# Weights read ahead, a norm chain in a fixed order and transposes moved among products, at the seam between an output projection and a SwiGLU FFN

## The chip, the core and the metric

The kernel runs on one core of a Trainium2 chip. The core has five engines with a queue each: PE (TensorE: matmuls and transposes into PSUM banks, and the loads of its stationary operand, which the profile lists apart as PEld), DVE (VectorE), ACT (ScalarE), POOL (GpSimd) and SP (SyncE, which here issues nearly all transfers). An engine takes the instructions of its queue in the order in which they stand; between engines, semaphores say when an operand is ready or a buffer is free. The metric is the device time of one execution in microseconds (us): the median of several runs.

## The reference

One encoder layer for 512 tokens of width 1024. Three mixers work on the same normalised input (sparse attention, stick-breaking attention, attention to memory), and their gated sum is `merged`. What the change touches comes after that:

```
x = x + rmsnorm(merged @ w_out, g_mix_post)
h = rmsnorm(x, g_ffn_pre)
gu = h @ w_ffn_in                       # 1024 x 5632
f = (silu(gu[:, :2816]) * gu[:, 2816:]) @ w_ffn_out
x = x + rmsnorm(f, g_ffn_post)
```

All values are float32.

## The kernel before, in words

A product in float32 is made of three products of rounded parts: each operand is split into a high part (a copy by ACT, `CAST` in the trace) and a low part (the difference, by DVE, `TENSOR_TENSOR`), and PE multiplies high by high, high by low, low by high (`passes`, `split`, `parts`). So each block of 512 KB of weights costs a transfer into a raw buffer (`wraw`, `lraw` or, after the change, `act`), a cast on ACT and a subtraction on DVE, each over 128x1024, before PE may use it. Buffers come from pools with a fixed number of places: `act` has 22, `wraw` 3, `lraw` 2, `wh` and `wl` 2 each, `w2` (both parts in one tile) 4. A split into a place that is taken waits until PE has used what is there. There are 8 PSUM banks.

`mix_out` (L785) multiplies the 512 tokens by `w_out` in two halves of 256 tokens; tokens come in tiles of 128, called 0 to 3 here. `w_out` has 8 blocks of 128 rows, k0 to k7, used alternately through a pair `wh`, `wl` (even blocks) and a `w2` tile (odd blocks). The first half runs k0 to k7 for tokens 0 and 1, twelve matmuls of 512 columns for a block; the splits of k4 to k7 are kept. The second half runs the kept blocks k4 to k7 first, then k0 and k1, which are loaded and split again, and at last k2 and k3 token by token (the tail, L755), so that token 2 is done before token 3. The split of k2 in the second half goes into the `wh`, `wl` pair of k6, and so has to wait until the second half has used k6.

When a token is done, `post_norm` (L767) takes squares of its two banks (ACT), a root (a small sum on DVE, a power on POOL, two small steps on DVE: `ms`, `rs`, `rt`), two products with the gain (DVE, `prod`) and two residual sums (DVE, `fin`); `normed` (L253) takes squares, root and a scaling (`xn`) of that for the FFN. Then `to_h2` (L797) transposes `xn` by PE, 16 transposes of 128x128 for two tokens, into a bank for each of 8 blocks of features, and ACT and DVE split each bank into `h2` (L78, L79). PE's order is written by hand throughout the kernel; that of ACT, DVE, POOL and SP is chosen by a scheduler when the program is built, except where a fixed order is asked for (`manual_schedule`).

The transposes of tokens 0 and 1 are handed out among the products of the second half: after more than `FT` (14) units of product, `FR` (0.65) of them for each further unit (L811). Past 17 units (`FW`, in the tail) the first three pairs of blocks of `w_ffn_in` are asked for (L809): raw buffers from `wraw` and `lraw`, parts in twelve `act` places; the low parts of three of the six blocks are meant for POOL, of which two stand there in the order of POOL's queue (L819 passes it for columns above 2816).

`ffn` (L932) multiplies the three pairs by the first half of `h2` (144 matmuls of 256 columns), then makes the last transposes (tokens 2 and 3), three steps ahead of the products of the first pair with the second half. What follows (L830 on) is a scheme with seven products for four blocks, whose left sides (`left_sides`, L851: sums and differences of weights, more splits) DVE and ACT prepare at the same time.

Of the kernel before, what the change touches and what calls it, by code (L numbers as in the profile page):

```python
# [27 lines left out]
TAKEN = -3.4e38  # L28
REL = 640
GA, GB = 2.05, 1.85  # L30
FS, FM, GC, FC, FA, FB, FW, FT, FR = 0.7, 50, 1.8, 2.0, 1.00, 2.20, 17.00, 14, 0.65

C_AQ, C_AK, C_AV, C_IQ, C_IK, C_BQ, C_BK, C_BV, C_CQ, C_G = (
    0, 512, 1024, 1536, 2048, 2120, 2632, 3144, 3656, 4168)
# [13 lines left out]
class Layer:  # L48
    def __init__(self, ctx, tc, a):
        self.tc, self.nc, self.a = tc, tc.nc, a  # L50
        self.queue, self.owed, self.nw, self.late = [], 0.0, 0, None
        pool = lambda name, **kw: ctx.enter_context(tc.tile_pool(name=name, bufs=1, **kw))
        self.pool = pool
        self.const = pool("const")
        self.sb = pool("sb")
        self.ps = pool("ps", space=bass.MemoryType.PSUM)
        self.dram = pool("dram", space=bass.MemoryType.DRAM)
# [162 lines left out]
                self.split(*out[t], ps)  # L220


    def squares(self, halves, both=False):

        ss = self.col("ss", 2)
        for c, x in enumerate(halves):
            junk = self.sb.tile([P, 512], F32, name="junk", tag="gate", bufs=2)
# [24 lines left out]

    def normed(self, x):  # L253

        r = self.rstd(self.squares([x[:, 0:512], x[:, 512:1024]]))
        xn = self.big("act", F32)
        self.scaled(xn, x, r)
        return xn


# [470 lines left out]
    def tok_pair(self, w_src, acts, nk, toks, tail=0, keep=0):  # L731

        pss = [[self.bank() for _ in range(2)] for _ in toks]
        kept, self.kept = self.kept, {}
        order = [*kept, *(k for k in range(nk) if k not in kept)]

        def one(k, w, t, ps, cs):
            wh, wl = w  # L740
            ah, al = acts[k]
            s = slice(t * P, (t + 1) * P)
            for st_, mv_, f, l in ((ah, wh, True, False), (ah, wl, False, False), (al, wh, False, True)):
                for c in cs:
# [22 lines left out]
    def post_norm(self, ps, grow, x, store=None):  # L767

        nc = self.nc
        r = self.rstd(self.squares(ps))  # L770
        ts = []
        for c in range(2):
            t = self.sb.tile([P, 512], F32, name="prod", tag="gate", bufs=2)
            nc.vector.scalar_tensor_tensor(t, ps[c], -0.5, grow[:, c * 512:(c + 1) * 512],
                                           op0=OP.mult, op1=OP.mult)
            ts.append(t)
        for c, t in enumerate(ts):
            s = slice(c * 512, (c + 1) * 512)
            nc.vector.scalar_tensor_tensor(x[:, s], t, r, x[:, s], op0=OP.mult, op1=OP.add)
            if store is not None:  # L780
                (nc.sync, nc.scalar)[c].dma_start(store[:, s], x[:, s])

    NFIRST = 3

    def mix_out(self):  # L785
        nc, a = self.nc, self.a
        gp = self.grow("g_mix_post", "act")
        self.h2 = [self.pair("h") for _ in range(NK)]
        self.x1 = [self.load_rows(a["x"], t, "fin") for t in range(NT)]
        xn = {}  # L790
# [12 lines left out]

        self.done, self.kept = done, {}
        for pr in range(2):
            us = 0.0
            for t in self.tok_pair(a["w_out"], self.mT, NK, (2 * pr, 2 * pr + 1), tail=2 * pr, keep=4 * (1 - pr)):
                us += t
                if pr == 1 and us > FW and not self.first_ffn:  # L809
                    self.first_ffn = [self.ffn_weights(j, ("act", "act")) for j in range(self.NFIRST)]  # L810
                if pr == 1 and us > FT:  # L811
                    self.fill(FR * t / 2.56)
            if pr == 0:
                self.add(to_h2(0))
        self.drain()
# [116 lines left out]
    def ffn(self):  # L932
# [28 lines left out]
        self.gated(pss, out(0))  # L961
        y = self.right_sides()
        for j, u in enumerate(first[1:], 1):
# [37 lines left out]
```

## Time and profile before

| | us |
|---|---|
| median of 3 runs | 912.44 (912.41 to 913.62) |
| the profiled execution, its own time | 910.88 |
| its span, first to last instruction | 909.1 |
| PE busy | 888.3 (98%) |
| DVE, ACT, POOL busy | 641.5, 458.6, 117.1 |

PE is busy nearly all the time, so the time is the sum of PE's work and of the places where PE waits. In the stretch that the change touches, from the first product with `w_out` at 503.5 us to the last transposes at 577.5 us, such places are found in the order of time of PE and PEld: a row there gives in brackets how long the engine sat idle before it and who ended that.

### The profile page before, as it was taken

Reading aid. Unit: us, or ns where it says so; the run is one execution under the profiler, and the core shown is the slowest. Engines: PE = TensorE matmul, PEld = TensorE weight load, DVE = VectorE, ACT = ScalarE, POOL = GpSimd, SP = SyncE. Lnnn points to the kernel's source line nnn. Section 1 sums busy time; section 2 is a strip of 40 time slices with the busy share of each in tenths; the row PEclk is TensorE's granted clock in tenths of the full one; section 3 lists DMA queues with packets and bytes.
Section 4 is the critical chain, followed back from the end, with each engine's and each line's share of the span. In section 5 each row is a group of like instructions: output and inputs, shape, how many; then the busy total and the mean of one; then the engine's idle time right before and its main releaser. Section 6 shows DMA issues by size and latency. Waiting matters only on the chain.

```text
span 909.1 us, 13518 instructions
## 1 busy us (share of the span) xinstructions
PE 888.3 (98%) x5146; PEld 780.1 (86%) x5146; DVE 641.5 (71%) x1120; ACT 458.6 (50%) x808; POOL 117.1 (13%) x153
## 2 busy tenths in 40 slices
PE   8999999999999999999999999899999999999997
PEld 7888888888888888888788888899999999888885
DVE  6589999953688976787563478788888887932215
ACT  6465674332666665666353355455555555811111
POOL 2000000020132304433212123400000000000000
PEclk9999999999999999999999999999999999999999
DMA  6523543454354433222483624213333334533002
GB/s 203 173 83 117 168 111 93 127 128 116 104 156 112 128 82 92 70 59 58 140 252 107 185 83 127 71 47 95 115 109 102 114 97 139 164 97 106 29 1 92
DMA packets 129541, 101.17 MB, mean 111 GB/s; under 512 B 4652, under 2 KB 115292, under 8 KB 129476
## 3 DMA queue, kind: packets, MB, share of 16 engines
q1 hardware_dynamic: 128884, 99.26, 37.9%
q10 hardware_dynamic: 592, 1.05, 0.3%
q8 instruction: 40, 0.66, 0.3%
q14 instruction: 25, 0.20, 0.1%
HBM read 93.73 MB, written 2.12 MB: 105 GB/s over the span
## 4 chain that ended last, share of the span: by engine, by line
PE 82%; DVE 10%; issue 3%; ACT 2%; POOL 2%; DMA 1%; POOLq 0%; DVEq 0%; ACTq 0%
PE bank L85 19%; PE bank L86 19%; PE bank L87 19%; PE bank L745 15%; DVE wl L75 3%; PE bank L545 2%; PE bank L560 1%; PE bank L179 1%; PE bank L178 1%; PE bank L209 1%; PE bank L211 1%; PE bank L210 1%; DMA lraw<-in_w_ffn_in_dram 1%; DVE e L632 1%; POOL rs L241 1%
## 5 line engine op out<-in xcount | busy, mean ns | idle before, releaser
L75 DVE TENSOR_TENSOR wl<-wraw,wh 128x1024 fp32r<-128x1024 f32 (+1 forms) x112 | 128.5, 1149 | 101.3 <-ACT wh L74 101.0
L74 ACT CAST wh<-wraw 128x1024 fp32r<-128x1024 f32 (+1 forms) x112 | 107.2, 959 | 139.3 <-PE bank L86 74.7
L85 PE MATMUL bank<-h,wh 128*128 128x512 f32 (+1 forms) x376 | 149.0, 396 | 0.0
L87 PE MATMUL bank<-h,wl 128*128 128x512 f32 (+1 forms) x376 | 145.4, 387 | 1.0 <-DVE wl L75 0.9
L86 PE MATMUL bank<-h,wh 128*128 128x512 f32 (+1 forms) x376 | 145.1, 386 | 0.0
L745 PE MATMUL bank<-w,act 128*128 128x512 f32 x360 | 89.0, 394 | 0.0
L87 PEld LDWEIGHTS bank<-h,wl 128*128 128x128 f32 x376 | 70.6, 188 | 15.8 <-DVE wl L75 1.7
L85 PEld LDWEIGHTS bank<-h,wh 128*128 128x128 f32 x376 | 71.0, 189 | 11.6 <-issue 0.2
L86 PEld LDWEIGHTS bank<-h,wh 128*128 128x128 f32 x376 | 70.9, 188 | 11.5
L745 PEld LDWEIGHTS bank<-w,act 128*128 128x128 f32 x360 | 67.4, 188 | 14.9
L745 PE MATMUL bank<-wh,act 128*128 128x512 f32 x240 | 72.5, 393 | 0.0
L85 PE MATMUL bank<-act,wh 128*128 128x256 f32 (+1 forms) x204 | 69.3, 340 | 0.7 <-DVE s L907 0.7
L86 PE MATMUL bank<-act,wh 128*128 128x256 f32 (+1 forms) x204 | 68.0, 334 | 0.0
L87 PE MATMUL bank<-act,w 128*128 128x256 f32 x228 | 64.2, 282 | 0.0
L86 PE MATMUL bank<-act,w 128*128 128x256 f32 x228 | 64.2, 281 | 0.0
L87 PE MATMUL bank<-h,w 128*128 128x256 f32 x228 | 64.2, 281 | 0.0
L86 PE MATMUL bank<-h,w 128*128 128x256 f32 x228 | 64.2, 281 | 0.0
L85 PE MATMUL bank<-act,w 128*128 128x256 f32 x228 | 64.2, 281 | 0.0
L85 PE MATMUL bank<-h,w 128*128 128x256 f32 x228 | 64.2, 281 | 0.0
L241 POOL TENSOR_TENSOR rs<-ms,mhalf 128x1 f32<-128x1 f32 x18 | 11.6, 646 | 387.4 <-DVE ms L240 383.7
L609 POOL TENSOR_TENSOR p<-toep,score 128x128 f32<-128x128 f32 (+3 forms) x32 | 30.4, 963 | 200.2 <-DVE score L518 102.9
L745 PEld LDWEIGHTS bank<-wh,act 128*128 128x128 f32 x240 | 45.0, 188 | 9.8
(190 smaller groups left out, 2109.5 us busy)
## 6 DMA issues: line engine op xcount, KB each, us to landing
wraw<-in_w_in_dram SPq DMA_DIRECT2D x64, 512.0 KB, 3.7
lraw<-in_w_ffn_in_dram SPq DMA_DIRECT2D x22, 512.0 KB, 4.0
wraw<-in_w_ffn_in_dram SPq DMA_DIRECT2D x22, 512.0 KB, 3.7
wraw<-in_w_ffn_out_dram SPq DMA_DIRECT2D x11, 512.0 KB, 3.5
lraw<-in_w_ffn_out_dram SPq DMA_DIRECT2D x11, 512.0 KB, 3.5
wraw<-in_w_mem_kv_dram SPq DMA_DIRECT2D x8, 512.0 KB, 3.7
lraw<-in_w_out_dram SPq DMA_DIRECT2D x6, 512.0 KB, 5.5
wraw<-in_w_out_dram SPq DMA_DIRECT2D x6, 512.0 KB, 3.9
```

What stands on the lines that cost most here:

```text
L74: self.nc.scalar.copy(hi, src)
L75: (eng or self.nc.vector).tensor_tensor(lo, src, hi.bitcast(F32), op=OP.subtract)
L85: self.nc.tensor.matmul(out, lhsT=sh, rhs=mh, start=first and i == 0, stop=False, **kw)
L86: self.nc.tensor.matmul(out, lhsT=sh, rhs=ml, start=False, stop=False, **kw)
L87: self.nc.tensor.matmul(out, lhsT=sl, rhs=mh, start=False, stop=last and i == n - 1, **kw)
L178: self.nc.tensor.matmul(out, lhsT=x, rhs=y[:, 0:n], start=True, stop=False)
L179: self.nc.tensor.matmul(out, lhsT=x, rhs=y[:, T:T + n], start=False, stop=True)
L209: self.nc.tensor.matmul(ps, lhsT=ah[:, s], rhs=wh[:, k2], start=st, stop=False)
L241: self.nc.gpsimd.tensor_tensor(r, ms, self.mhalf, op=OP.pow)
L545: self.nc.tensor.transpose(ps[:, c:c + P], p[i][:, j * P:(j + 1) * P], self.ident)
L609: nc.gpsimd.tensor_tensor(s, toep[0][:, 0:n][:, ::-1], self.mask[i], op=OP.add)
L745: self.nc.tensor.matmul(ps[c], lhsT=st_[:, s], rhs=mv_[:, 0, c * 512:(c + 1) * 512], start=f and k == order[0], stop=l and k == order[-1])
```

## The change

- `ffn_weights` reads its raw block into an `act` place instead of `wraw` or `lraw`, and all low parts are made by DVE. The three pairs are asked for in the first half of `w_out`, after more than 4, 9 and 14 units (`FW`).
- The transposes of tokens 0 and 1 begin after 12 units instead of 14 (`FT`), one unit for each unit of product (`FR`).
- From the tail of the second half on (`tail`, called ahead of the loads of k2 and k3) until the first pair's products with the second half are issued, ACT, DVE and POOL keep the order in which the program is written (`manual_schedule`), and the norm chain of tokens 2 and 3 is written out step by step in it (`done`, `ends`).
- The squares write what nobody reads into `xn`, not into the two `gate` buffers; one of the two squares of `normed` for tokens 2 and 3 is done by DVE (`both`).
- The first three steps of the last transposes stand among the products: one after six of eight pieces of the third pair with the first half, one at its end, one ahead of the first pair's products with the second half.

```
-FS, FM, GC, FC, FA, FB, FW, FT, FR = 0.7, 50, 1.8, 2.0, 1.00, 2.20, 17.00, 14, 0.65
+FS, FM, GC, FC, FA, FB, FT, FR = 0.7, 50, 1.8, 2.0, 1.00, 2.20, 12, 1.0
+FW = 4, 9, 14, 99
...
+        if self.tail:
+            self.tail()
         ws = {k: load(k) for k in order[nk - tail:]}
...
+        def square(t):
+            xn[t] = self.big("act", F32)
+            ss[t] = self.squares(bank[t], to=xn[t])
...
+        def ends():
+            square(3)
+            prods(3)
+            root(3)
+            square2(2)
+            root(2)
+            residual(3)
+            square2(3)
+            scale(2)
+            root(3)
+            scale(3)
+
+        order = lambda: self.tc.manual_schedule(engines={
+            mybir.EngineType.DVE, mybir.EngineType.Activation, mybir.EngineType.Pool})
...
         def done(t, ps):
-            self.post_norm(ps, gp, self.x1[t])
-            xn[t] = self.normed(self.x1[t])
+            bank[t] = ps
+            if t < 2:
+                self.post_norm(ps, gp, self.x1[t])
+                xn[t] = self.normed(self.x1[t])
+            if t == 2:
+                square(2)
+                prods(2)
+                root(2)
+                residual(2)
+            if t == 3:
+                ends()
...
+        def tail():
+            self.ordered.enter_context(order())
...
-                if pr == 1 and us > FW and not self.first_ffn:
-                    self.first_ffn = [self.ffn_weights(j, ("act", "act")) for j in range(self.NFIRST)]
+                if pr == 0 and us > FW[len(self.first_ffn)]:
+                    self.first_ffn.append(self.ffn_weights(len(self.first_ffn)))
...
-    def ffn_weights(self, j, tags=None):
-        return [self.parts(self.load(self.a["w_ffn_in"][:, c:c + P], NK, P), tags, self.nc.gpsimd if tags and c>DFF else None) for c in (j * P, DFF + j * P)]
+    def ffn_weights(self, j):
+        return [self.parts(self.load(self.a["w_ffn_in"][:, c:c + P], NK, P, "act"), ("act", "act"))
+                for c in (j * P, DFF + j * P)]
...
-            run(products(*u, 0))
+            for i, _ in enumerate(products(*u, 0)):
+                if j == self.NFIRST - 1 and i in (5, 7):
+                    next(self.last_h2)
...
-        for k in range(NK + 2):
-            if k < NK:
+        for k in range(NK):
+            if k + 2 < NK:
                 next(self.last_h2)
-            if k > 1:
-                for ps, w in zip(pss, ws):
-                    self.feat_k(ps[:, 256:512], w, self.h2, k - 2, n=256, t0=256)
+            for ps, w in zip(pss, ws):
+                self.feat_k(ps[:, 256:512], w, self.h2, k, n=256, t0=256)
+        self.ordered.close()
```

**PE, second half of `w_out`.** Before, from the block k0 (`wh`, `wl`) and k1 (`w_5395`) to the start of the tail (k3 is `w_5433`); `ident` marks a transpose:

```order
L745 MATMUL bank<-wh,act 128x512 x2
L745 MATMUL bank<-w_5395,act 128x512 x12
L359 MATMUL bank<-ident,act 128x128 x6
L745 MATMUL bank<-wh,act 128x512
L745 MATMUL bank<-wl,act 128x512
```

and with the change:

```order
L750 MATMUL bank<-wh,act 128x512 x2
L364 MATMUL bank<-ident,act 128x128 x8
L750 MATMUL bank<-w_5447,act 128x512 x12
L364 MATMUL bank<-ident,act 128x128 x8
L750 MATMUL bank<-wh,act 128x512
```

The transposes of tokens 0 and 1 stand one block earlier, eight ahead of the twelve matmuls of k1 and eight behind; before, six followed k1 and ten were spread over the tail.

**ACT, from the squares of token 0's banks to the first squares for token 1's `xn`.** With buffer numbers; `junk` and `act_5313`, `act_5343` are what the squares write, `fin_5107` and `fin_5109` the residual sums of tokens 0 and 1, `bank_5115` to `bank_5118` their banks. Before (`wh_5377` is k0's cast, `wh_5427` k2's):

```order
L231 ACTIVATE junk_5262,ss_5259<-bank_5116 128x512
L231 ACTIVATE junk_5278,ss_5277<-fin_5107 128x512
L231 ACTIVATE junk_5280,ss_5277<-fin_5107 128x512
L231 ACTIVATE junk_5292,ss_5291<-bank_5117 128x512
L231 ACTIVATE junk_5294,ss_5291<-bank_5118 128x512
L74 CAST wh_5377<-wraw_5375 128x1024
L231 ACTIVATE junk_5310,ss_5309<-fin_5109 128x512
L74 CAST wh_5427<-wraw_5425 128x1024
```

With the change (`wh_5409` is k0's cast, `wh_5486` k2's, `w2_5492` k3's; `act_5250` and `act_5256` belong to the third FFN pair, `w2_5961` and `wh_5976` to the left sides of the next):

```order
L237 ACTIVATE junk_5298,ss_5295<-bank_5116 128x512
L76 CAST wh_5409<-wraw_5407 128x1024
L76 CAST act_5250<-act_5248 128x1024
L76 CAST wh_5486<-wraw_5484 128x1024
L76 CAST act_5256<-act_5254 128x1024
L76 CAST w2_5492<-lraw_5490 128x1024
L237 ACTIVATE act_5313,ss_5314<-fin_5107 128x512 x2
L237 ACTIVATE junk_5326,ss_5325<-bank_5117 128x512
L237 ACTIVATE junk_5328,ss_5325<-bank_5118 128x512
L76 CAST w2_5961<-wraw_5957 128x1024
L76 CAST wh_5976<-lraw_5959 128x512
L237 ACTIVATE act_5343,ss_5344<-fin_5109 128x512 x2
```

Five casts moved ahead of the squares of token 0's residual sum and two more ahead of those of token 1's; DVE has the five low parts in the same place (`wl`, `act`, `wl`, `act`, `w2`).

**DVE, the end of the norm chain of tokens 2 and 3.** Before, from the scaling of token 3 (L251) to the first split of the last transposes (L79); `wl_6069`, `wl_6070` and `wh_6081` are left sides of a later block:

```order
L251 TENSOR_SCALAR act_5583<-fin_5113,rs_5577 128x1024
L871 TENSOR_TENSOR wl_6069<-lraw_6064 128x512
L871 TENSOR_TENSOR wl_6070<-wraw_6062,lraw_6064 128x512
L871 TENSOR_TENSOR wl_6069<-wl_6069,wraw_6062 128x512
L75 TENSOR_TENSOR wh_6081<-lraw_6064,wh_6081 128x512
L871 TENSOR_TENSOR wl_6070<-wraw_6062,wl_6069 128x512
L79 SCALAR_TENSOR_TENSOR h_5099<-bank_5735,cols_96,h_5099 128x256
```

With the change:

```order
L938 TENSOR_TENSOR wl_6061<-wraw_6053,wl_6060 128x512
L257 TENSOR_SCALAR act_5507<-fin_5111,rs_5552 128x1024
L246 TENSOR_SCALAR ms_5567<-ss_5560 128x1
L77 TENSOR_TENSOR wh_6072<-lraw_6055,wh_6072 128x512
L252 SCALAR_TENSOR_TENSOR rt_5571<-rs_5568,ms_5567 128x1
L253 SCALAR_TENSOR_TENSOR rs_5568<-rt_5571,rs_5568 128x1
L257 TENSOR_SCALAR act_5536<-fin_5113,rs_5568 128x1024
L81 SCALAR_TENSOR_TENSOR h_5099<-bank_5713,cols_96,h_5099 128x256
```

The five operations on left sides that stood between the last scaling and the first split now stand ahead of it.

## Rows read from the trace of the kernel before

**Rows 1.** The page: busy time of PE, share of the span, instructions.

```profile
PE 888.3 (98%) x5146; PEld 780.1 (86%) x5146; DVE 641.5 (71%) x1120; ACT 458.6 (50%) x808; POOL 117.1 (13%) x153
```

**Rows 2.** PEld in order of time: start us, us, instruction [idle before <- who ended it].

```profile
547.27 0.20 PEld L359 LDWEIGHTS bank<-ident,act 128*128 128x128 f32 x2 [1.97 <-DVE h L79]
...
569.39 0.31 PEld L359 LDWEIGHTS bank<-ident,act 128*128 128x128 f32 x3 [0.40 <-DVE act L251]
572.80 0.20 PEld L359 LDWEIGHTS bank<-ident,act 128*128 128x128 f32 x2 [3.09 <-DVE h L79]
```

**Rows 3.** DVE in order of time, at the two places where PE waits.

```profile
539.30 0.75 DVE L251 TENSOR_SCALAR act<-fin,rs 128x1024 f32<-128x1024 f32 x1
539.97 1.22 DVE L75 TENSOR_TENSOR act<-wraw,act 128x1024 fp32r<-128x1024 f32 x1
...
542.24 4.58 DVE L75 TENSOR_TENSOR act<-wraw,act 128x1024 fp32r<-128x1024 f32 x2
546.74 1.65 DVE L79 SCALAR_TENSOR_TENSOR h<-bank,cols,h 128x256 fp32r<-128x256 f32 x4
...
569.25 0.69 DVE L871 TENSOR_TENSOR wl<-lraw 128x512 f32<-128x512 f32 x1
```

**Rows 4.** PE in order of time: k7 and k1 of the second half, first FFN product.

```profile
534.30 2.93 PE L745 MATMUL bank<-w,act 128*128 128x512 f32 x12
...
539.84 2.93 PE L745 MATMUL bank<-w,act 128*128 128x512 f32 x12
...
551.68 0.28 PE L85 MATMUL bank<-h,act 128*128 128x256 f32 x1
551.80 0.28 PE L86 MATMUL bank<-h,act 128*128 128x256 f32 x1
```

**Rows 5.** ACT in order of time: squares of token 0's sum, of token 1's banks, casts.

```profile
528.08 0.63 ACT L231 ACTIVATE junk<-fin 128x512 f32<-128x512 f32 x1 [2.22 <-DVE fin L779]
...
529.37 0.58 ACT L231 ACTIVATE junk<-bank 128x512 f32<-128x512 f32 x1
...
530.51 1.05 ACT L74 CAST wh<-wraw 128x1024 fp32r<-128x1024 f32 x1
...
537.34 1.03 ACT L74 CAST act<-wraw 128x1024 fp32r<-128x1024 f32 x1
538.28 1.04 ACT L74 CAST act<-lraw 128x1024 fp32r<-128x1024 f32 x1
```

**Rows 6.** DVE in order of time: residual sums, and from a root's first step to its next.

```profile
527.24 1.41 DVE L779 SCALAR_TENSOR_TENSOR fin<-prod,rs,fin 128x512 f32<-128x512 f32 x2
...
529.50 0.21 DVE L240 TENSOR_SCALAR ms<-ss 128x1 f32<-128x1 f32 x1 [0.85 <-ACT junk L231]
530.38 0.22 DVE L246 SCALAR_TENSOR_TENSOR rt<-rs,ms 128x1 f32<-128x1 f32 x1 [0.66 <-POOL rs L241]
...
564.86 0.21 DVE L240 TENSOR_SCALAR ms<-ss 128x1 f32<-128x1 f32 x1
...
566.64 0.22 DVE L246 SCALAR_TENSOR_TENSOR rt<-rs,ms 128x1 f32<-128x1 f32 x1 [0.44 <-POOL rs L241]
```

**Rows 7.** Windows at the end: length, then busy of PE, PEld, DVE, ACT, POOL, granted clock, DMA.

```profile
902.00:904.00 2.00, 0.36 (x2) 0.00 (x0) 0.81 (x2) 0.69 (x2) 0.53 (x1) 1.00 0.00 0
904.00:906.00 2.00, 0.00 (x0) 0.00 (x0) 1.79 (x4) 0.00 (x0) 0.02 (x1) 0.98 0.00 0
906.00:909.00 3.00, 0.00 (x0) 0.00 (x0) 0.00 (x0) 0.00 (x0) 0.00 (x0) 0.50 0.46 175
```

**Rows 8.** PE in order of time at the kernel's start: transposes of a constant.

```profile
1.66 1.33 PE L400 MATMUL bank<-ident 128*128 128x128 f32 x5 [1.66 <-POOL mhalf L324]
...
3.12 3.31 PE L400 MATMUL bank<-ident 128*128 128x128 f32 x21
...
8.04 1.25 PE L400 MATMUL bank<-ident 128*128 128x128 f32 x10
```

**Rows 9.** The page: transfers of w_ffn_in, count, KB each, median us to landing.

```profile
lraw<-in_w_ffn_in_dram SPq DMA_DIRECT2D x22, 512.0 KB, 4.0
```

More of the change, by code (lines that the diff above doesn't have):

```diff
@@ L50, in __init__ @@
         self.tc, self.nc, self.a = tc, tc.nc, a
-        self.queue, self.owed, self.nw, self.late = [], 0.0, 0, None
+        self.queue, self.owed, self.nw, self.late, self.tail = [], 0.0, 0, None, None
+        self.ordered = ExitStack()
         pool = lambda name, **kw: ctx.enter_context(tc.tile_pool(name=name, bufs=1, **kw))
@@ L220, in tok_tiles, with squares @@
                 self.split(*out[t], ps)
-    def squares(self, halves, both=False):
+    def squares(self, halves, both=False, to=None):
         ss = self.col("ss", 2)
         for c, x in enumerate(halves):
-            junk = self.sb.tile([P, 512], F32, name="junk", tag="gate", bufs=2)
+            if to is None:
+                junk = self.sb.tile([P, 512], F32, name="junk", tag="gate", bufs=2)
+            else:
+                junk = to[:, c * 512:(c + 1) * 512]
             if both and c:
@@ L253, in normed @@
     def normed(self, x):
-        r = self.rstd(self.squares([x[:, 0:512], x[:, 512:1024]]))
         xn = self.big("act", F32)
-        self.scaled(xn, x, r)
+        self.scaled(xn, x, self.rstd(self.squares([x[:, 0:512], x[:, 512:1024]], to=xn)))
         return xn
@@ L765, in tok_pair, with prods @@
                 self.done(t, ps)
-    def post_norm(self, ps, grow, x, store=None):
-        nc = self.nc
-        r = self.rstd(self.squares(ps))
+    def prods(self, ps, grow):
         ts = []
@@ L773, in post_norm, with residual @@
             t = self.sb.tile([P, 512], F32, name="prod", tag="gate", bufs=2)
-            nc.vector.scalar_tensor_tensor(t, ps[c], -0.5, grow[:, c * 512:(c + 1) * 512],
-                                           op0=OP.mult, op1=OP.mult)
+            self.nc.vector.scalar_tensor_tensor(t, ps[c], -0.5, grow[:, c * 512:(c + 1) * 512],
+                                                op0=OP.mult, op1=OP.mult)
             ts.append(t)
+        return ts
+    def residual(self, ts, r, x, store=None):
+        nc = self.nc
         for c, t in enumerate(ts):
@@ L781, in post_norm @@
                 (nc.sync, nc.scalar)[c].dma_start(store[:, s], x[:, s])
+    def post_norm(self, ps, grow, x, store=None):
+        r = self.rstd(self.squares(ps))
+        self.residual(self.prods(ps, grow), r, x, store)
     NFIRST = 3
@@ L789, in mix_out, with prods, root, residual @@
         self.x1 = [self.load_rows(a["x"], t, "fin") for t in range(NT)]
-        xn = {}
+        xn, ss, r, ts, bank = {}, {}, {}, {}, {}
         self.first_ffn = []
-        def done(t, ps):
-            self.post_norm(ps, gp, self.x1[t])
-            xn[t] = self.normed(self.x1[t])
+        def square(t):
+            xn[t] = self.big("act", F32)
+            ss[t] = self.squares(bank[t], to=xn[t])
+        def prods(t):
+            ts[t] = self.prods(bank[t], gp)
+        def root(t):
+            r[t] = self.rstd1(ss[t])
+        def residual(t):
+            self.residual(ts[t], self.rstd2(r[t]), self.x1[t])
+        def square2(t):
+            x = self.x1[t]
+            ss[t] = self.squares([x[:, 0:512], x[:, 512:1024]], both=True, to=xn[t])
+        def scale(t):
+            self.scaled(xn[t], self.x1[t], self.rstd2(r[t]))
+        def ends():
[11 more added lines that the diff above has]
+            mybir.EngineType.DVE, mybir.EngineType.Activation, mybir.EngineType.Pool})
+        def done(t, ps):
+            bank[t] = ps
[9 more added lines that the diff above has]
+                ends()
         def to_h2(pr):
@@ L802, in to_h2 @@
                 yield 0.25
-        self.done, self.kept = done, {}
+        def tail():
+            self.ordered.enter_context(order())
+        self.done, self.kept, self.tail = done, {}, None
         for pr in range(2):
             us = 0.0
+            if pr == 1:
+                self.tail = tail
             for t in self.tok_pair(a["w_out"], self.mT, NK, (2 * pr, 2 * pr + 1), tail=2 * pr, keep=4 * (1 - pr)):
                 us += t
-                if pr == 1 and us > FW and not self.first_ffn:
-                    self.first_ffn = [self.ffn_weights(j, ("act", "act")) for j in range(self.NFIRST)]
+                if pr == 0 and us > FW[len(self.first_ffn)]:
+                    self.first_ffn.append(self.ffn_weights(len(self.first_ffn)))
                 if pr == 1 and us > FT:
@@ L814, in mix_out @@
                 self.add(to_h2(0))
+        self.tail = None
         self.drain()
         self.last_h2 = to_h2(1)
-    def ffn_weights(self, j, tags=None):
-        return [self.parts(self.load(self.a["w_ffn_in"][:, c:c + P], NK, P), tags, self.nc.gpsimd if tags and c>DFF else None) for c in (j * P, DFF + j * P)]
+    def ffn_weights(self, j):
+        return [self.parts(self.load(self.a["w_ffn_in"][:, c:c + P], NK, P, "act"), ("act", "act"))
+                for c in (j * P, DFF + j * P)]
     def right_sides(self):
```

## The prediction

> **What bounds the kernel now.** I read the page first: PE is busy for 98% of the span [rows 1], so only two things can change the time, the work that PE has and the places where it stands still. The change gives PE the same matmuls and transposes in another order, so I looked for the stops. PEld in order of time shows three between 503.5 and 577.5 us [rows 2]: 1.97 us ahead of the transposes at 547.27, and 0.40 and 3.09 us in the last transposes, at 569.39 and 572.80, together 5.46 us. The reader is to see in the brackets who ended each: a split of an earlier transpose (`h`, L79) on DVE twice, and once the scaling of token 3. DVE in order of time says why those were late [rows 3]. At 546.74 the first four splits start, behind four low parts of FFN weights that stood ahead of them, of which the last two took 4.58 us instead of twice 1.22. At 569.25 begins a run of five operations on left sides, 0.69 us each, which nothing in these transposes needs, and the split comes behind it.
>
> **The change, part by part.** Durations are those of the profiled execution, 910.88 us, 1.56 below the median of 912.44; I work out a difference and put it on the median. In the chains below I count whole durations and leave out the one-column steps; a follower starts a little before its predecessor's end, and that about pays for them.
>
> *Loads and splits of the three pairs.* They move to the first half of `w_out`. A load of 512 KB lands 4.0 us after its issue [rows 9]; six of them, two of left sides and the gain go out in some 20 us, and the last two casts are not in the first half but behind the squares of token 0. Two blocks take PE 5.54 us, k7's start to k1's [rows 4], so the eight of the first half 22 us, and the four casts and splits put there take 3.8 us of ACT's (0.94 each [rows 5]) and 4.9 of DVE's (1.22 [rows 3]): nothing on the path. One of the loads passes those of k0 and k2 on SP's queue, which are wanted no earlier than 534; behind them stand the loads of later blocks. The 4.58 us of the two slow low parts goes, and so the cause of the first stop.
>
> *The transposes of tokens 0 and 1.* They now stand ahead of k1 of the second half, where PE arrives when it starts k1 today, at 539.84 [rows 4]. Before, the scaling of token 1 ended at 540.05 [rows 3], while PE was at k1. So the question is when it ends now, and that is read from the order of ACT: the casts of k0, k2 and k3 of the second half and the last two of the third pair stand ahead of the squares of token 0's sum. The cast of k2 writes where the kept k6 is, so it cannot start until PE is through with k6 in the second half: k7 starts at 534.30 [rows 4], k6's last matmul ends about 0.16 later, at 534.5. ACT takes its queue in order, so the squares that ran at 528.08 [rows 5] are held behind it. From there, step by step:
> - three casts, 0.94 us from one start to the next [rows 5]: 537.3;
> - squares of token 0's sum, 529.37 less 528.08 [rows 5]: 538.6; squares of token 1's banks, 530.51 less 529.37 [rows 5]: 539.75;
> - DVE waits with the second product of token 1 for these, 0.69 (a 128x512 operation [rows 3]): 540.4; scaling of token 0, 0.75 [rows 3]: 541.2; token 1's root, 0.88 from its first step to the next [rows 6], is done meanwhile;
> - a weight split of a later block, 1.22 [rows 3], and a left side, 0.69, stand ahead of the residual sums: 543.1; two residual sums, 1.41 [rows 6]: 544.5;
> - two more left-side operations, 1.38, under which ACT does token 1's squares: 545.9; root, 0.88: 546.8; one more weight split, 1.22: 548.0; scaling, 0.75: 548.7.
>
> PE stands from 539.84 to 548.7, 8.9 us, where 1.97 us was lost before: **plus 6.9 us**. Bounds: with the overlaps of eleven followers, some 0.08 each (539.97 against 540.05 [rows 3]), and no one-column step it ends at 547.9 (plus 6.1). With the two roots that are on the path at 1.78, as one took while DVE was full [rows 6], it ends at 550.5 (plus 8.7). I take 548.7, since the root at 529.50 is the one with the same neighbours.
>
> *The norm chain of tokens 2 and 3 and the last transposes.* From the end of the tail, T, PE has 132 matmuls of 256 columns at 0.12 from start to start [rows 4] before the first of these transposes: it arrives at T + 15.8. DVE has in its order from T on eleven operations over 128x512 at 0.69 (seven for left sides, two products, two squares), two pairs of residual sums at 1.41, two weight splits at 1.22 and two scalings at 0.75 [rows 3, 6]: 14.35, and 0.2 more in the last root, 14.5 us. So the scaling ends 1.3 us before PE comes, and the splits then have an empty queue. The 0.40 and 3.09 us [rows 2] go: **minus 3.5 us**. One step of squares per token moves from ACT to DVE and the unread results to `xn`; both lie inside the 14.5. The cover is that margin of 1.3 us; if it is gone, a wait of up to 3.5 us stays.
>
> *The clock after the long stop.* When PE ends at the kernel's end, early in the window from 902, the granted clock is 1.00, 0.98 in the window from 904 and 0.50, the lower of its two levels, from 906 on [rows 7]: it had fallen within 4 us of the last matmul. The new stop is twice as long, with one transpose (token 0) inside, so I expect PE to start again at 1.2 GHz. What that costs no stop of this trace shows. The nearest rows are the opening: 26 transposes from 1.66 to 6.43, against 0.11 from start to start in the ten at 8.04 [rows 8]: 4.5 us instead of 2.9. That is 1.6 us lost, an estimate, because other things start there too. Below it is zero (the clock does not fall), above it 3.6 us, if the twelve matmuls of k1 (2.77 us) and eight transposes (0.9) ran at half pace. I take **plus 1.6**. The Trainium skill ("TensorE: Matmul & The Clock Gate", Part 1) calls the lower clock the default that activity lifts, and has an idle stretch bring it back; by that rule the 1.6 belongs into the sum and the edit pays for its stop twice, and without it the sum is 3.4.
>
> Sum: 6.9 - 3.5 + 1.6 = 5.0 us. On the profiled execution 915.9, on the median **917.4 us**.
>
> **Rivals.**
> *The clock stays up.* The stop of 3.09 us [rows 2] was followed by matmuls at full pace, and one transpose of token 0 stands inside the new one. Then 912.44 + 3.4 = 915.8. Chance 0.2.
> *The margin at the last transposes is gone.* POOL's powers slow down beside a full DVE (1.78 for a root [rows 6]), and token 2's chain can start late. Then 3.5 us is lost again: 920.9. Chance 0.15.
> *Loads hold ACT.* Four casts of the first half stand ahead of the squares of token 0; if their loads took twice the 4.0 us [rows 9], ACT would reach the squares late. The cast of k2 waits until 534.5 anyway, so this adds something only past some 8 us. In that sense the change would not do what it says; 918 to 920. Chance 0.03.
> *Faster.* The squares of token 0 are not held, token 1 is scaled by 540 as before, and both stops vanish: 912.44 - 5.5 = 907.0. It decides at 545.3, where the new first stop costs just what the two old ones did. For it: DVE is free of the slow 4.58 us, and the early splits leave ACT less to do there. Against: the order of ACT with the cast of k2 in front, and a buffer that PE frees at 534.5; even then 10.8 us of chain would have to become less than 5.5. Chance 0.08.
> *A draw* between those, with the scaling at about 545: 912.4. Chance 0.04.
>
> **How the numbers follow.** Forecast 0.5, the others as given. Slower by over 0.2% (1.8 us, about what a measurement of this kernel can tell from no change): 0.5 + 0.2 + 0.15 + 0.03 = 0.88; within 0.2%: 0.04; faster: 0.08. The range takes the bounds: below 6.1 - 3.5 + 0 = 2.6, which is 915.0, less half a us for the spread of the runs; above 8.7 - 3.5 + 3.6 = 8.8, which is 921.2. So 914.5 to 921.5; it holds the forecast, the first two rivals and most of the third.
>
> **What would show it.** PEld's idle before the second transpose of the second half of `w_out` some 7 to 10 us long and ended by DVE's scaling; ACT's cast of k2 right ahead of token 0's squares, begun near 534.5; the granted clock below 1.00 in a window behind that stop; no idle above 0.5 us in the last transposes. The prediction is wrong if token 1's scaling ends before 545, if the first stop is short although the cast of k2 waits, or if the time of the seam falls with the stop still there.

## The result and the profile after the change

The changed kernel takes 917.31 us (median of 4 runs, 916.56 to 917.55) against 912.42 us for the kernel before on the same chip (4 runs, 910.44 to 913.62). The ratio is 1.0054 with a 95% interval of 1.0036 to 1.0073: **slower, by about half a per cent**, 4.9 us. The profiled execution took 917.3 us and has a span of 915.5, where the one before had 909.1. In the runs of the kernel before that stand beside the experiments, the time goes with the mean granted clock that each run lists: 910.75 to 910.96 us at 0.998, 912.02 to 912.99 at 0.996 or 0.997, 913.29 to 913.93 at 0.995; the profiled execution of before, 910.88 us at 0.998, belongs to the shortest.

The page's busy line answers to [rows 1]: PE has the same 5146 instructions and is busy 2.9 us longer, although its work is the same.

```profile
PE 891.2 (97%) x5146; PEld 783.1 (86%) x5146; DVE 644.2 (70%) x1126; ACT 458.3 (50%) x804; POOL 111.5 (12%) x151
```

PEld of the kernel after in order of time: the rows at transposes that have an idle time in brackets, from 538 to 590, and the first row of the last transposes (576.94), which has none. They answer to [rows 2].

```profile
541.71 0.14 PEld L364 LDWEIGHTS bank<-ident,act 128*128 128x128 f32 x1 [2.11 <-ACT wh L76]
...
549.18 1.35 PEld L364 LDWEIGHTS bank<-ident,act 128*128 128x128 f32 x7 [7.33 <-issue]
...
576.94 0.24 PEld L364 LDWEIGHTS bank<-ident,act 128*128 128x128 f32 x2
...
580.16 0.20 PEld L364 LDWEIGHTS bank<-ident,act 128*128 128x128 f32 x2 [0.36 <-DVE h L81]
```

The first stop is now 2.11 + 7.33 = 9.44 us, with the one transpose of token 0 in the middle; before it was 1.97. In the last transposes 0.36 us is left of 0.40 + 3.09. That is 7.47 more and 3.13 less, 4.34 together. The rest of the 6.4 us between the two spans, some 2 us, is in PE's pace behind the stop, as `busy_stop` below shows. PE of the kernel after in order of time, to be held against the 2.93 us of k1's twelve matmuls in [rows 4]:

```profile
549.21 1.73 PE L364 MATMUL bank<-ident,act 128*128 128x128 f32 x7 [7.16 <-DVE act L257]
550.59 4.32 PE L750 MATMUL bank<-w,act 128*128 128x512 f32 x12
554.75 1.04 PE L364 MATMUL bank<-ident,act 128*128 128x128 f32 x8
```

and the windows around it (length, then busy of PE, PEld, DVE, ACT, POOL, granted clock, DMA share, GB/s):

```profile
540.00:542.00 2.00, 0.28 (x2) 0.14 (x1) 2.00 (x8) 1.32 (x2) 0.55 (x1) 1.00 0.77 224
542.00:544.00 2.00, 0.04 (x1) 0.00 (x0) 2.00 (x4) 0.00 (x0) 0.00 (x0) 0.79 0.16 47
544.00:546.00 2.00, 0.00 (x0) 0.00 (x0) 2.00 (x5) 1.71 (x5) 0.00 (x0) 0.50 0.00 0
...
550.00:552.00 2.00, 2.00 (x8) 1.72 (x7) 1.76 (x4) 1.45 (x4) 0.00 (x0) 0.50 0.00 0
552.00:554.00 2.00, 2.00 (x7) 1.60 (x6) 0.00 (x0) 0.00 (x0) 0.00 (x0) 0.65 0.00 0
554.00:556.00 2.00, 2.00 (x14) 1.74 (x14) 0.33 (x1) 0.83 (x3) 0.00 (x0) 1.00 0.00 0
```

The granted clock goes to 0.50, the lower of its two levels, while PE stands, and is still there when PE starts again at 549.2; it is back at 1.00 only in the window from 554. k1 takes 4.32 us in place of 2.93.

Why PE stood is read on ACT and DVE. ACT of the kernel after in order of time:

```profile
529.96 1.05 ACT L76 CAST act<-act 128x1024 fp32r<-128x1024 f32 x1
534.53 1.05 ACT L76 CAST wh<-wraw 128x1024 fp32r<-128x1024 f32 x1 [3.53 <-PE bank L750]
535.49 1.05 ACT L76 CAST act<-act 128x1024 fp32r<-128x1024 f32 x1
536.44 1.04 ACT L76 CAST w<-lraw 128x1024 fp32r<-128x1024 f32 x1
537.38 0.63 ACT L237 ACTIVATE act<-fin 128x512 f32<-128x512 f32 x1
```

The second row is the cast of k2. It stands for 3.53 us until a matmul of PE (the last that reads the kept k6) ends, and the squares of token 0's residual sum, which ran at 528.08 before [rows 5], come behind it and two further casts at 537.38. DVE then has token 1's chain between weight splits and left sides of later blocks:

```profile
541.64 1.22 DVE L77 TENSOR_TENSOR w<-wraw,w 128x1024 fp32r<-128x1024 f32 x1
...
542.85 0.68 DVE L938 TENSOR_TENSOR wl<-lraw 128x512 f32<-128x512 f32 x1
543.45 1.41 DVE L789 SCALAR_TENSOR_TENSOR fin<-prod,rs,fin 128x512 f32<-128x512 f32 x2
544.78 0.68 DVE L938 TENSOR_TENSOR wl<-wl,wraw 128x512 f32<-128x512 f32 x1
545.38 0.68 DVE L77 TENSOR_TENSOR wh<-lraw,wh 128x512 fp32r<-128x512 f32 x1
...
546.85 0.22 DVE L252 SCALAR_TENSOR_TENSOR rt<-rs,ms 128x1 f32<-128x1 f32 x1 [0.66 <-POOL rs L247]
...
547.18 1.22 DVE L77 TENSOR_TENSOR w<-wl,w 128x1024 fp32r<-128x1024 f32 x1
548.31 0.75 DVE L257 TENSOR_SCALAR act<-fin,rs 128x1024 f32<-128x1024 f32 x1
```

The last row is the scaling of token 1; it ends at 549.06, and PE goes on at 549.18.

### The profile page after: what moved, and what is told of

The parts are those of the page before. It is cut to its first block, busy times and chain, and to the rows that moved or that the text cites. A ratio compares the mean times of both kernels' runs of the same rounds, so it can differ in the third digit from the quotient of the medians.

```text
span 915.5 us, 13518 instructions
## 1 busy us (share of the span) xinstructions
PE 891.2 (97%) x5146; PEld 783.1 (86%) x5146; DVE 644.2 (70%) x1126; ACT 458.3 (50%) x804; POOL 111.5 (12%) x151
## 4 chain that ended last, share of the span: by engine, by line
PE 86%; DVE 8%; issue 2%; ACT 2%; POOL 1%; DMA 0%; POOLq 0%; DVEq 0%; ACTq 0%
PE bank L87 19%; PE bank L88 19%; PE bank L89 19%; PE bank L750 17%; DVE wl L77 3%; PE bank L550 2%; PE bank L565 1%; PE bank L181 1%; PE bank L180 1%; PE bank L211 1%; PE bank L213 1%; PE bank L212 1%; DVE e L637 1%; DVE score L522 1%; PE bank L364 1%
```

## The experiments

The theory: the cast of k2 ahead of token 0's squares holds ACT until PE is done with k6, and that makes the first stop; the granted clock, which falls in it, adds some 2 us. Rivals: work of later blocks on DVE sets the end of the chain; the transposes stand a block too early in any order; the fixed order is what shifted the casts. The first four kernels were run together, then the next four, then the last two, each set on a chip of its own beside runs of the kernel before (medians 912.47, 912.45 and 912.30), which agree to 0.2 us.

### The chain of tokens 0 and 1 first, then k2 (chain_first, k2_ahead, k2_ahead_no_wait)

In `chain_first` the chain of tokens 0 and 1 is written step by step inside the region of fixed order (`order()`), between the blocks of the second half; `get(k)` loads and splits block k of `w_out`, `sq(t)` squares a residual sum on ACT. The keys 1, 2, 3 are the number of blocks of the second half whose matmuls have been issued.

```diff
-FW = 4, 9, 14, 99
+FW = 4, 9, 99
...
+        self.prev = kept
...
-            if t < 2:
-                self.post_norm(ps, gp, self.x1[t])
-                xn[t] = self.normed(self.x1[t])
+            if t == 1:
+                self.ordered.enter_context(order())
+                square(0)
+                prods(0)
+                root(0)
+                square(1)
+                residual(0)
...
+        def get(k):
+            self.prev[k] = self.weights(a["w_out"][k * P:(k + 1) * P, :], 1, 1024)
+
+        pre = {
+            1: lambda: (sq(0), prods(1), root(1), get(0), residual(1), root(0), sq(1), scale(0)),
+            2: lambda: (root(1), get(1), scale(1)),
+            3: lambda: (get(2), get(3)),
+        }
...
+                if pr == 1:
+                    n += 1
+                    pre.get(n, int)()
+                    if n == max(pre):
+                        self.ordered.close()
+                        self.first_ffn.append(self.ffn_weights(2))
```

> The norm chain of tokens 0 and 1 stands in a fixed order on ACT, DVE and POOL, with the casts of k0 and k1 where they fit in and those of k2 and k3 behind it; the third FFN pair is read behind the chain; the transposes stay where the change put them. Theory (the cast of k2 ahead of the squares of token 0's sum makes the first stop): the squares start near 528.5 instead of 535.5 or later, token 1 is scaled by about 540, and PE's first stop falls from 9.4 us (2.11 + 7.33) to under 1.5; the clock stays at 1.00, the stops of the last transposes stay away. Time 912.4 - 5.5 + 0.5 to 1.5 = 907.5 to 908.5. Rival, work of later blocks on DVE (weight splits and left sides) sets the end of the scaling: the stop stays at 4 us or more, 911 or above. Rival, the transposes stand a block too early whatever the order: stop of 3 us or more, 910 or above.

Measured: 907.71 us (907.54 to 907.83, 5 runs), ratio 0.9950 [0.9937, 0.9962]. PEld of `chain_first` in order of time has one stop at the first transposes, the first row here:

```profile
540.89 0.75 PEld L364 LDWEIGHTS bank<-ident,act 128*128 128x128 f32 x7 [1.11 <-issue]
...
567.46 0.14 PEld L364 LDWEIGHTS bank<-ident,act 128*128 128x128 f32 x1 [0.64 <-issue]
```

(the second row is a stop of the last transposes, which the change does not have), and ACT does the first squares of token 0's sum at 528.71, released by DVE's residual sum and held by no cast:

```profile
528.71 0.63 ACT L237 ACTIVATE act<-fin 128x512 f32<-128x512 f32 x1 [1.45 <-DVE fin L790]
```

The transposes stand where the change put them, three weight pairs are still read early (the third a little later), and the stop is 1.11 us in place of 9.44. So the early place of the transposes is not the cause; the order is. Weight splits still stand between the steps of the chain on DVE here and cost no more than this 1.11.

`k2_ahead` takes the same kernel and moves only the steps, so that k0, k1 and, last, k2 come ahead of the squares:

```diff
+            1: lambda: (get(0)),
+            2: lambda: (get(1)),
+            3: lambda: (get(2), sq(0), prods(1), root(1), residual(1), root(0), sq(1), scale(0), root(1), scale(1), get(3)),
```

> As chain_first, but the casts of k0, k1 and k2, in this order, stand ahead of the squares of token 0's sum in the fixed order; k2 writes where the kept k6 is. Theory: ACT stands at the cast of k2 until PE is through with k6 near 534.5, the squares follow at 535.5, and the stop at the first transposes is 5 to 8 us again; with the clock's loss the time is 914 to 917. Rival, left sides and splits on DVE are what counts: the same as chain_first within 2 us.

Measured: 915.59 us (914.87 to 915.89, 5 runs), ratio 1.0034 [1.0022, 1.0047]. ACT of `k2_ahead` in order of time:

```profile
534.45 1.05 ACT L76 CAST wh<-wraw 128x1024 fp32r<-128x1024 f32 x1 [2.58 <-PE bank L751]
535.41 0.62 ACT L237 ACTIVATE act<-fin 128x512 f32<-128x512 f32 x1
```

and PEld:

```profile
545.01 0.18 PEld L364 LDWEIGHTS bank<-ident,act 128*128 128x128 f32 x1 [5.49 <-ACT w L76]
547.00 1.35 PEld L364 LDWEIGHTS bank<-ident,act 128*128 128x128 f32 x7 [1.81 <-ACT w L76]
```

The stop is back with 7.30 us (5.49 + 1.81), and the granted clock falls in it:

```profile
546.00:548.00 2.00, 0.97 (x5) 1.00 (x6) 1.96 (x3) 0.60 (x3) 0.00 (x0) 0.50 0.00 0
```

So 7.9 us of time came with this order alone.

`k2_ahead_no_wait` has the same order but reads k1 late in the chain, ahead of the scaling of token 1, so that k2 falls on the pool `w2`, which has a free buffer, and k1 on the pair of k6, free by then:

```diff
+            1: lambda: (get(0)),
+            3: lambda: (get(2), sq(0), prods(1), root(1), residual(1), root(0), sq(1), scale(0), root(1), get(1), scale(1), get(3)),
```

> As k2_ahead, but k1 is read behind the chain, so k2's turn falls on the other set of buffers, which has a free one: its cast stands ahead of the squares and waits only for its load. Theory (the wait for k6 is the cost, not the cast itself): the cast of k2 starts near 530, the squares near 531.5, and the stop is 2 to 4 us, which gives 909.5 to 911.5. Rival, the place of the cast in the queue is the cost, with or without the wait: as k2_ahead, 914 or more.

Measured: 911.21 us (909.58 to 912.35, 10 runs), ratio 0.9987 [0.9978, 0.9996]. The profiled execution is the shortest of the ten. Its stop, and a window in which PE stands still (the granted clock is the 1.00 ahead of the DMA share):

```profile
543.57 0.74 PEld L364 LDWEIGHTS bank<-ident,act 128*128 128x128 f32 x7 [3.91 <-issue]
```

```profile
540.00:542.00 2.00, 0.01 (x1) 0.00 (x0) 1.56 (x5) 2.00 (x3) 0.72 (x1) 1.00 0.12 35
```

ACT of this kernel in order of time:

```profile
529.83 1.05 ACT L76 CAST w<-lraw 128x1024 fp32r<-128x1024 f32 x1
530.77 0.63 ACT L237 ACTIVATE act<-fin 128x512 f32<-128x512 f32 x1
```

The cast of k2 starts at 529.83 and the squares follow at 530.77, 4.64 us earlier than in `k2_ahead`. By the medians, 4.4 of the 7.9 us between `chain_first` and `k2_ahead` go with the wait for k6's buffer, and 3.5 are left for the longer queue in and ahead of the chain. By the spans of the profiled executions (905.9, 907.8 and 913.5) it is 5.7 and 1.9. The split is so uncertain because of the clock: in the profiled execution of `k2_ahead_no_wait` the stop leaves it at 1.00, with a mean of 0.998, but eight of the ten executions list 0.995 to 0.997. The share of k1's cast, which is out of the way too, was not measured apart from that of the wait.

### The clock (busy_stop)

```diff
         for t, x in enumerate(xs):
+            if t and self.warm:
+                for _ in range(self.warm):
+                    self.nc.tensor.transpose(ps[:, P:2 * P], self.ident, self.ident)
+                self.warm = 0
             self.nc.tensor.transpose(ps[:, t * P:(t + 1) * P], x[:, k * P:(k + 1) * P], self.ident)
...
             if pr == 0:
+                self.warm = 60
                 self.add(to_h2(0))
```

> The changed kernel with 60 more transposes of the constant between the first transpose of token 0 and the first of token 1, where PE stands for 7.3 us: at 0.115 us each they take 6.9 us, and their result is overwritten. Theory (the clock falls in the stop, and PE then works at half pace for 3.4 us): with PE busy the granted clock stays at 1.00 over the stop, k1's twelve matmuls take 2.9 us instead of 4.3, and the time falls by 1.5 to 2.2 us against the change, to 915.1 to 915.8. Rival, the longer k1 has another cause, or the stop itself is the whole cost: 917.3 unchanged, or later, if the added transposes outlast the stop.

Measured: 915.44 us (915.21 to 915.62, 5 runs), ratio 1.0034 [1.0022, 1.0047], and so 1.9 us less than the changed kernel's 917.31 with 60 instructions more. PE of `busy_stop` in order of time:

```profile
541.89 6.71 PE L366 MATMUL bank<-ident 128*128 128x128 f32 x60
549.22 0.95 PE L368 MATMUL bank<-ident,act 128*128 128x128 f32 x7 [0.61 <-DVE act L257]
549.93 3.02 PE L754 MATMUL bank<-w,act 128*128 128x512 f32 x12
```

The seven transposes begin at 549.22, as in the changed kernel (549.21): the stop is as long. The next matmuls start 0.71 us later in place of 1.38, k1 takes 3.02 in place of 4.32. Two of the windows:

```profile
544.00:546.00 2.00, 2.00 (x21) 2.00 (x20) 2.00 (x5) 1.70 (x5) 0.00 (x0) 1.00 0.00 0
...
550.00:552.00 2.00, 2.00 (x11) 1.65 (x10) 1.66 (x4) 1.12 (x4) 0.00 (x0) 1.00 0.00 0
```

The clock's share of the loss is shown: 1.9 us by the medians, 2.0 by the spans of the profiled executions (915.5 and 913.5).

### Which part of the change did it (loads_only, loads_as_before, no_fixed_order, last_in_a_row)

`loads_only`: both groups of transposes back, no fixed order. Of the change it keeps the early loads, the squares that write to `xn` and the norm chain of tokens 2 and 3 in its new form.

```diff
-FS, FM, GC, FC, FA, FB, FT, FR = 0.7, 50, 1.8, 2.0, 1.00, 2.20, 12, 1.0
+FS, FM, GC, FC, FA, FB, FT, FR = 0.7, 50, 1.8, 2.0, 1.00, 2.20, 14, 0.65
...
-            self.ordered.enter_context(order())
+            pass
...
-            for i, _ in enumerate(products(*u, 0)):
...
+            run(products(*u, 0))
```

(and the loop over k in `ffn` as before the change; both are shown at `last_in_a_row`).

> Of the change only the early reading of the three FFN weight pairs (and the squares' results going to xn): no fixed order, and both groups of transposes where they stood before. In this program too the cast of k2 stands ahead of the squares of token 0's sum on ACT. Theory (the early reading is what lets that cast go ahead, and the cast makes the stop): ACT stands there until 534.5, token 1 is scaled near 548.5, PE comes to the first transposes 2.8 us later than in the changed kernel (k1's matmuls stand ahead) and so stands 5 to 6.5 us; about 1 us is lost at the last transposes; with 0 to 2 us for the clock the time is 912.4 - 5.5 + 6 to 9.5 = 913 to 916.5, slower than before. Rival, the earlier place of the first transposes makes the loss: 912 or below.

Measured: 914.16 us (913.65 to 914.78, 8 runs), ratio 1.0023 [1.0013, 1.0033]. PEld of `loads_only`, its stop at the first transposes:

```profile
548.17 0.93 PEld L364 LDWEIGHTS bank<-ident,act 128*128 128x128 f32 x5 [5.62 <-issue]
```

and what its waits by line say of all transposes from 500 to 600 (in total, times, longest):

```profile
PEld bank L364 <- issue: 5.8, 2, 5.6
PEld bank L364 <- DVE h L81: 1.1, 1, 1.1
```

ACT of `loads_only` in order of time, the cast of k2 and the first squares of token 0's sum:

```profile
534.54 1.05 ACT L76 CAST wh<-wraw 128x1024 fp32r<-128x1024 f32 x1 [1.72 <-PE bank L750]
536.70 1.05 ACT L76 CAST act<-act 128x1024 fp32r<-128x1024 f32 x1 [1.11 <-DMA act<-in_w_ffn_in_dram]
537.66 0.63 ACT L237 ACTIVATE act<-fin 128x512 f32<-128x512 f32 x1
```

With the early loads and neither new place nor fixed order, the long stop is there; of the two parts that are kept besides, `loads_as_before` below shows that they do not bring it. Behind k2's cast ACT waits here another 1.11 us for a load of the third FFN pair, so an early load can hold ACT too. The old stop at the last transposes is mostly gone: 1.1 us is left of 3.49.

`loads_as_before`: the changed kernel with `FW`, `ffn_weights` and their call as in the kernel before.

```diff
-FW = 4, 9, 14, 99
+FW = 17.0
...
-                if pr == 0 and us > FW[len(self.first_ffn)]:
-                    self.first_ffn.append(self.ffn_weights(len(self.first_ffn)))
+                if pr == 1 and us > FW and not self.first_ffn:
+                    self.first_ffn = [self.ffn_weights(j, ("act", "act")) for j in range(self.NFIRST)]
```

> The changed kernel with the three FFN weight pairs read as before, in the second half; the transposes' new places and the fixed order stay. In this program the squares of token 0's sum stand ahead of the casts of k0 and k2. Theory: ACT does them near 528, token 1 is scaled at 541 to 543, so that the first stop is 1 to 3.5 us in place of 9.4; the FFN splits then delay the chain of tokens 2 and 3, which gives 1 to 4 us at the last transposes; 909.5 to 914. Rival, the earlier place of the first transposes makes the 9.4 us whatever is read when: 916 or more.

Measured: 914.88 us (914.37 to 916.03, 6 runs), ratio 1.0031 [1.0019, 1.0043]: above the 914 that I gave the theory and below the 916 of its rival. Its stops on PEld:

```profile
542.63 0.75 PEld L364 LDWEIGHTS bank<-ident,act 128*128 128x128 f32 x7 [1.70 <-ACT act L76]
...
571.54 0.18 PEld L364 LDWEIGHTS bank<-ident,act 128*128 128x128 f32 x1 [3.07 <-issue]
574.39 0.18 PEld L364 LDWEIGHTS bank<-ident,act 128*128 128x128 f32 x1 [2.66 <-issue]
```

ACT does the squares of token 0's sum early again, ahead of the casts of k0 and k2:

```profile
529.21 0.63 ACT L237 ACTIVATE act<-fin 128x512 f32<-128x512 f32 x1 [2.16 <-DVE fin L789]
```

The first stop is 1.70 us with the transposes in their new place, as the theory has it. What I had put too low is the end: 3.07 + 2.66 = 5.73 us at the last transposes, although the chain of tokens 2 and 3 is in its fixed order and the transposes stand among products. The granted clock falls there besides:

```profile
572.00:574.00 2.00, 0.02 (x1) 0.00 (x0) 1.52 (x5) 0.00 (x0) 0.56 (x1) 0.50 0.20 57
574.00:576.00 2.00, 1.58 (x8) 1.61 (x9) 0.76 (x2) 0.47 (x1) 0.03 (x1) 0.50 0.94 278
```

and the matmuls behind that stop begin 0.21 us apart in place of 0.12. So part of what this kernel loses is the clock's. Without the early loads the two other parts together do not help; each alone was not tried without them.

`no_fixed_order`:

```diff
-            self.ordered.enter_context(order())
+            pass
```

> The changed kernel without the fixed order of the norm chain of tokens 2 and 3. Theory (the first stop comes from the early loads, and the stop in the last transposes goes because the left sides no longer stand at the end of DVE's queue): the first stop stays 8.5 to 9.5 us; if the left sides are back behind the last scaling, 1.5 to 3.5 us come back at the last transposes, 918.5 to 921; if the chain has enough lead without the order, 916.5 to 917.5. Rival, the fixed order is what puts the casts ahead of the squares: the first stop falls below 4 us and the time below 913.

Measured: 916.54 us (916.27 to 917.17, 5 runs), ratio 1.0052 [1.0040, 1.0065]. The first stop is 2.11 + 6.34 us, with the cast of k2 at 534.68 and the squares of token 0's sum at 537.82; at the last transposes 0.4 us is left, as with the order. So the fixed order did not shift k2's cast and did not remove the stop at the end.

`last_in_a_row`: only the transposes' place in `ffn` is undone.

```diff
-            for i, _ in enumerate(products(*u, 0)):
-                if j == self.NFIRST - 1 and i in (5, 7):
-                    next(self.last_h2)
+            run(products(*u, 0))
...
-        for k in range(NK):
-            if k + 2 < NK:
+        for k in range(NK + 2):
+            if k < NK:
                 next(self.last_h2)
-            for ps, w in zip(pss, ws):
-                self.feat_k(ps[:, 256:512], w, self.h2, k, n=256, t0=256)
+            if k > 1:
+                for ps, w in zip(pss, ws):
+                    self.feat_k(ps[:, 256:512], w, self.h2, k - 2, n=256, t0=256)
```

> The changed kernel with the last transposes in a row ahead of the products that read them, as before; the rest as in the change, the fixed order too. Theory (the order of DVE, with an empty queue behind the last scaling, took the 3.09 us away; standing among products hides the first split): PE waits some 1 us for the first split again, 918 to 918.6. Rival, the place among the products alone took the 3.5 us away: 920.5 or more.

Measured: 918.51 us (918.21 to 918.73, 5 runs), ratio 1.0073 [1.0060, 1.0085], 1.2 us more than the changed kernel. From its waits by line:

```profile
PEld bank L364 <- DVE h L81: 1.1, 1, 1.1
```

The place among products hides the first split, 0.7 us of wait by the profile (1.1 in place of 0.36).

### What beats both (chain_first_tail_free, chain_first_later)

`chain_first_tail_free` is `chain_first` with the body of `tail()` empty, `chain_first_later` has the bound of 14 in place of 12 for the first transposes besides. Against `chain_first`:

```diff
         def tail():
-            self.ordered.enter_context(order())
+            pass
...
-FS, FM, GC, FC, FA, FB, FT, FR = 0.7, 50, 1.8, 2.0, 1.00, 2.20, 12, 1.0
+FS, FM, GC, FC, FA, FB, FT, FR = 0.7, 50, 1.8, 2.0, 1.00, 2.20, 14, 1.0
```

> chain_first without the fixed order of the chain of tokens 2 and 3. The stop of 9.4 us, under which DVE could catch up in the other kernels, is not there, so this tells whether the fixed order is wanted. Theory (the early loads and the places among products took the 3.5 us away, the fixed order adds nothing): no stop above 0.7 us at the last transposes, 906.8 to 907.9. Rival, without the order the left sides end up ahead of the last scalings or splits: a stop of 1.5 to 3.5 us there, 909 to 911.

> chain_first_tail_free with the first transposes behind k1's matmuls instead of ahead of them, a bound of 14 us in place of 12. Theory (what is left of the first stop, 1.11 us, is token 1's scaling at 540.9 against PE's arrival at 539.6): with PE 2.8 us later it goes, 905.8 to 906.8. Rival, the later transposes give later splits and a stop of over 1 us at the end of the tail or at the first FFN product: 907.5 or more.

Measured: 907.02 us (906.99 to 907.40, 5 runs), ratio 0.9945 [0.9932, 0.9957], and 906.50 us (906.45 to 906.77, 5 runs), ratio 0.9938 [0.9925, 0.9952]. The fixed order of the last chain isn't wanted even where no long stop lets DVE catch up: without it the time is 0.7 us lower, and the wait of 0.64 us that `chain_first` has in the last transposes is gone. With the later transposes the waits of PEld at transposes are

```profile
PEld bank L364 <- DVE h L81: 1.2, 3, 0.8
```

of which no part is token 1's scaling. This version is 5.8 us below the kernel before beside it and 10.8 below the change.

## Why the prediction came out

Forecast 917.4, range 914.5 to 921.5; measured 917.31. The end is right to 0.1 us, the terms are not: against the span, which rose by 6.4 us, the sum of 5.0 was 1.4 too small. That it meets the median is luck. The profiled execution of before, from which the terms were read, is 1.56 us below its own median and has a mean granted clock of 0.998, where the runs near that median, as far as their clock is listed, have 0.996 or 0.997; that of after (917.30) lies on its median. So the median of before holds about as much lost to the clock as the sum was short of, and the prediction had no term for it. Where in the kernel that clock is lost, no trace shows. The three kernels built on `chain_first`, whose longest stop at these transposes is 1.11 us, list 0.998 or 0.999 in every run; that points to the stops of before, but is not shown.

- **The first stop, plus 6.9: right in cause, 0.6 low.** The chain ran as it was read from ACT's order: cast of k2 at 534.53 (534.5 predicted), squares of token 0 at 537.38 (537.3), token 0 scaled at 541.59 (541.2), residual sums of token 1 done at 544.86 (544.5), token 1 scaled at 549.06 (548.7). PE came to the transposes some 0.2 us earlier than taken, and the stop was 9.44 us (8.9). The pair `chain_first` and `k2_ahead` shows the cause.
- **The last transposes, minus 3.5: right in size, wrong in what does it.** Minus 3.13 was measured. Token 3 is scaled at 575.74 and PE's first transpose is loaded at 576.94, a margin of 1.2 us (1.3 predicted). But the working put this under the norm chain in fixed order with an empty queue behind it. `no_fixed_order` keeps the gain, `loads_as_before` loses it all with the order in place, and `loads_only` has 1.1 us left: the early loads bring most of it, and the place among products the last 0.7 to 1.2 us. With the early loads no split of the three pairs stands on DVE behind 538; that this is how they do it was not tested apart.
- **The clock, plus 1.6: right, a little low.** It is 1.9 us by `busy_stop`. The Trainium skill ("TensorE: Matmul & The Clock Gate", Part 1), by which an idle stretch brings the lower clock back, agrees with the 0.50 from 544 on in the kernel after and with the 1.00 of `busy_stop`.
- **Loads and splits of the three pairs, booked at nothing: the step that failed in its reasoning.** Their transfers and their work were hidden, as said. But `loads_only` gives the stop and `loads_as_before` doesn't: with their moving the casts of k0 and k2 come to stand ahead of the squares. Why the scheduler then chooses so was not looked into. The prediction read the consequence off the order and charged it to the transposes.
- **The rivals.** The clock did not stay up; the margin at the end was not gone; the loads did not hold ACT in the change (its long waits ahead of the squares are for PE), only in `loads_only` and `no_fixed_order`, by 1.1 us. The faster case is what `chain_first` then is, at 907.71 against 907.0 given for it; in the change itself the squares were held, as argued against it. That argument has a slip: by the prediction's own steps the chain behind 534.5 is 14.2 us long (548.7 less 534.5); 10.8 is the length at which the two sides would balance, at 545.3.

## What to carry to other kernels

ACT took its queue in order here, and a cast that waited 3.53 us for a buffer held everything behind it: look, for each operation on the path, at what stands ahead of it and when the buffer that this one writes comes free. An edit whose own work is hidden can still be the dear one, if the scheduler then puts something that waits ahead of the path; undo each part alone before a gain or a loss is put down to one. And a long stop of PE costs more than its length where the granted clock falls in it: here 1.9 us on top of 9.44.

## What was not expected of the hardware

- The length of a stop alone did not decide whether PE's clock fell in it. In the profiled execution of `k2_ahead_no_wait`, with a stop of 3.91 us, the granted clock is 1.00 in every window from 538 to 556, and in that of the kernel before it is 1.00 from 566 to 578, over the stop of 3.09. In `loads_as_before` it falls between 571.0 and 571.5, inside a stop of 3.07 us that ends at 571.54. Executions of one kernel differ as well: those of `k2_ahead_no_wait` go from 909.58 us at a mean of 0.998 to 912.35 at 0.995. The prediction had only weighed whether a stop lowers the clock, not that like stops differ.
- Sixty transposes of a constant in a stop that can't be avoided gave back 1.9 us, at no cost that the runs show: the stop behind them still ended at 549.2.
- The two splits of FFN weights that took 4.58 us on DVE before [rows 3] have their like where those loads stay in the second half: in `loads_as_before` one low part of 128x1024 takes 3.28 us at 551.47. With the early loads they are gone from this stretch. POOL makes a low part of its own at the same time (2.44 us from 551.23); whether that slows them was not tried.
